# Residual kept in HBM, a second pair of raw-split buffers, and a fixed issue order on two engines, in a float32 encoder block on one Trainium2 core

## The chip, the cores and the metric

The kernel runs on one core of one Trainium2 chip. The time is device microseconds (us) of one execution; it is given as the median of three runs, with the lowest and highest. A profiled execution, recorded by the hardware profiler, has its own time and a span, from the first recorded instruction to the last. The engines are named as in the profile: PE is TensorE (its matmuls; PEld is its weight loads), DVE is VectorE, ACT is ScalarE, POOL is GpSimd and SP is SyncE, which issues the DMAs. L289 means line 289 of the kernel whose profile is shown.

## The reference

One encoder block on x of 256 tokens by 2048 channels, in float32. Cut to what matters:

```python
def swiglu(h, w_gate, w_up, w_down):
    return (jax.nn.silu(h @ w_gate) * (h @ w_up)) @ w_down

for l in range(DEPTH):                                    # DEPTH = 1
    x = x + 0.5 * swiglu(rms_norm(x, ffn1_norm[l]), ffn1_w_gate[l], ffn1_w_up[l], ffn1_w_down[l])
    h = rms_norm(x, mix_norm[l])
    proj = h @ w_in[l]
    ...
    x = x + jnp.concatenate([y_pool, y_gla], axis=-1) @ w_out[l]
    x = x + mem_cross_attention(rms_norm(x, xattn_norm[l]), rms_norm(mem, mem_norm[l]),
                                xattn_w_q[l], xattn_w_kv[l], xattn_w_o[l])
    x = x + 0.5 * swiglu(rms_norm(x, ffn2_norm[l]), ffn2_w_gate[l], ffn2_w_up[l], ffn2_w_down[l])
return rms_norm(x, final_norm)
```

The gate and up weights are 2048 x 5632, the down weights 5632 x 2048. Each value of x is changed seven times by a projection before the last down projection: the residual x is what the change moves.

## The kernel before

**Float32 products out of rounded halves.** PE multiplies values of a shorter float32 form (fp32r in the profile). Each float32 operand is therefore split into a rounded high part and a low remainder, and a product is made of three matmuls: high by high, high by low, low by high. `split` (L215) does this with two instructions: a cast on ACT (L216) and a subtraction on DVE (L217). Activations are split once into `xs` (the normalized x, transposed) or `ys` (the hidden values, transposed); weights are split as they stream in.

**Units.** The weights come in units of 1 MB. A unit u has a raw tile (tag `raw`, three buffers), loaded by SP (L471), and its parts `wh` and `wl` (three buffers each). `Stream.emit` writes the program out: before the matmuls of unit u it calls `prepare(u + 3)`, the split of unit u + 2, and the load of unit u + 5. There are 378 units. Units 0 to 131 are the first feed-forward (FFN1), 246 to 377 the second (FFN2); between them lie the mixer's w_in, w_out (166 to 181), the cross attention and w_o (230 to 245).

**Plain and seven-product units.** A plain unit of a feed-forward (`block_t`, L291, and `unit_p`, L409) has 24 matmuls. Units 0, 2 and 4 of most gate and up blocks of eight units, 54 units in all, save an eighth of them: the 2 x 2 block product is made with seven products in place of eight (`seven`, L367, matmuls at L383), 21 matmuls. Such a unit needs sums of its weight blocks: `add_weights` makes them in tile `T` with three DVE instructions (L345, L348, L349), ahead of the split, in `prepare`. `split_seven` splits T into th and tl, which lie in `wh` and `wl`, and the last three quarters of the raw tile into `xh` and `xl`, which have one buffer each. That second split is a function `rest`, which `emit` calls at the start of the next step, and the load of the raw tile's successor stands behind it.

**A block's end.** A seven-product block needs four accumulators (tiles of PSUM, of which there are four of two banks, tag `ps`). After the last seven-product unit `combine` (L421) moves two of them together into an `sg` tile; after the last unit of the block `join` (L432) adds the other two, and then `ev_gate` applies silu on ACT (L628) or `ev_up` multiplies on DVE (L633). `turn` (L638) transposes a finished half on PE (L643, eight transposes) and splits it into `ys`.

**The feed-forward's order.** `ffn` (L614) goes through three parts of the 5632 hidden columns, (0, 4), (4, 4) and (8, 3) in blocks of 512. A part runs gate and up blocks for two 512-column blocks at a time, g0 u0 g2 u2 in the first part, g4 u4 g6 u6 in the second, g8 u8 and a mixed gate/up block in the third, and then its down projection. In units of FFN1: g0 0 to 7, u0 8 to 15, g2 16 to 23, u2 24 to 31, down 32 to 47, g4 48 to 55, u4 56 to 63, g6 64 to 71, u6 72 to 79, down 80 to 95, and so on. The halves of u0 and u4 are turned six units after their block, so at the end of g2 and g6 (`wait`, L658); the halves of u2 and u6 one unit after theirs.

**The residual.** `X` (L167) holds all of x in SBUF for the whole run, 16 KB in each partition. `residual` (L557) adds the accumulators of a down projection, w_out or w_o into it on DVE (L561). `into_x` (L583) runs two blocks of 1024 columns, b = 0 and 1; where a norm follows, `fold` (L566) transposes the new x on PE into `xs` and takes its squares. The last down projection (`down_end`, L1105) adds, normalizes and stores the output.

**Who sets the order.** A planner places the written instructions on each engine's queue by costs of its own, within what the data allow. An engine then issues its queue in order and waits at an instruction whose inputs are not there. `tc.keep_in_program_order` holds an instruction in the written order with its like. The pools of the scopes (`scope["pool"]`) hold xh, xl, T, `sg` and others; a buffer is taken again when its last reader is done.

Of the kernel before, what the change touches and what calls it, by code (L numbers as in the profile page):

```python
# [7 lines left out]
F32 = mybir.dt.float32  # L8
# [6 lines left out]
P = 128  # L15
D = 2048
# [73 lines left out]
            f(*w.pop(u))  # L90


def build(ctx, tc, I, out):
    nc = tc.nc
    st = Stream()

    head = ctx.enter_context(tc.tile_pool(name="head", bufs=1))
# [22 lines left out]
    def four(ps):  # L120
        return ps.rearrange("p a (b c) -> p (a b) c", c=S)
# [29 lines left out]


    ident = head.tile([P, P], F32, tag="ident", name="ident")
    make_identity(nc, ident)
    ones = const.tile([P, P], F32, tag="ones", name="ones")
    nc.vector.memset(ones, 1.0)
    invc = ctl("invc", [P, PAD])
# [6 lines left out]
    sums = ctl("sums", [P, 2])  # L164
    chain = ctl("chain", [P, 2, 8])

    X = main.tile([P, 2, D], F32, tag="X", name="X")  # L167
    xs = main.tile([P, KT, 2, S], F32R, tag="xs", name="xs")
    ys = main.tile([P, KT, 2, S], F32R, tag="ys", name="ys")

# [51 lines left out]
    def row_squares(src, c):  # L222

        for h in range(2):
            j = tmp.tile([P, S], F32, tag="j", name=uid("j"), bufs=2)
            nc.scalar.activation(j, src[h], AF.Square, accum_out=ss[:, h, c : c + 1])
# [125 lines left out]
    def split_seven(u, raw, t):  # L352
        th, tl = (
            wpool.tile([P, 4 * NB], F32R, tag=n, name=f"{n}{u}", bufs=st.AHEAD + 1)
            for n in ("wh", "wl")
        )
        split(th, tl, t)
        parts = [x.rearrange("p (b n) -> p b n", n=NB) for x in (th, tl)]

        def rest():  # L360
            r = [scope["pool"].tile([P, 3 * NB], F32R, tag=n, name=f"{n}{u}") for n in ("xh", "xl")]
            split(*r, raw[:, NB:])
            parts.extend(x.rearrange("p (b n) -> p b n", n=NB) for x in r)

        return [parts], rest

    def seven(banks, act, ext, i, g, first, later, weights):  # L367
        th, tl, rh, rl = weights
# [150 lines left out]
    def turn_gains(lo, hi):  # L519
        ps = ptile(uid("pgain"))  # L520
        nc.tensor.transpose(ps[:, 0, :P], rows["gain"], ident)
        nc.vector.tensor_copy(gains[:, lo:hi], ps[:, 0, lo:hi])

    def load_x(c):
        cols = slice(c * S, (c + 1) * S)
        nc.sync.dma_start(X[:, :, cols], I["x"][0].rearrange("(h p) d -> p h d", p=P)[:, :, cols])

    def first_load_order():
        for c in range(1, 8):
# [2 lines left out]

    first_loads = first_load_order()

    def x_chunk(c):
        v = ptile(uid("px"))[:, 0, :].rearrange("p (a b) -> p a b", a=2)
        k = 2 * c
        for j in range(2):
            for h in range(2):
                nc.tensor.transpose(  # L540
                    v[:, j, h * P : (h + 1) * P], X[:, h, (k + j) * P : (k + j + 1) * P], ident
                )
        for j in range(2):
            rows["hi", c] = split_scaled(xs, k + j, v[:, j, :], gcol(G_FFN1 + k + j))

    def x_squares(c):
        with tc.issue_after(rows["hi", c].ins):
            row_squares([X[:, h, c * S : (c + 1) * S] for h in range(2)], c)

    def more_gains():  # L550
        gain_columns(
# [2 lines left out]
             ("gla_b_a", G_BA, 4)], nc.sync,  # L554
        )

    def residual(scale, b):  # L557

        def evict(j, ps):
            x = X[:, :, (2 * b + j) * NB : (2 * b + j + 1) * NB]  # L560
            nc.vector.scalar_tensor_tensor(  # L561
                out=x, in0=ps, scalar=scale, in1=x, op0=ALU.mult, op1=ALU.add
            )
        return evict

    def fold(c, gain):  # L566

        v = four(ptile(uid("px")))
        for j in range(4):
            for h in range(2):  # L570
                nc.tensor.transpose(  # L571
                    v[:, j, h * P : (h + 1) * P],
                    X[:, h, c * NB + j * P : c * NB + (j + 1) * P], ident,
                )
        for j in range(4):
            split_scaled(xs, 4 * c + j, v[:, j, :], gcol(gain + 4 * c + j))
        for h in range(2):
            q = tmp.tile([P, NB], F32, tag="j", name=uid("j"), bufs=2)
            nc.scalar.activation(
                q, X[:, h, c * NB : (c + 1) * NB], AF.Square, accum_out=ss[:, h, c : c + 1]  # L580
            )

    def into_x(w, act, scale, gain=None, k0=0, nk=KT, spread_too=True):  # L583

        for b in range(2):
            block_t(wwide(w, b * 2 * NB, k0, nk), act, residual(scale, b))
            if gain is not None:
                for j in range(2):
                    st.op(lambda c=2 * b + j: fold(c, gain), 1)
        if gain is not None:  # L590
            st.op(lambda: finish_norm(4, spread_too), 2)
            if spread_too:
                st.op(spread_norm, 3)
# [14 lines left out]
    class Ext:  # L608


        def __getitem__(self, i):
            return rows["xe"][i]

    def ffn(wg, wu, wd, down):  # L614
        gate = {}

        def hidden():
            e = scope["pool"].tile([P, 4, NB], F32, tag="sg", name=uid("sg"), bufs=2)
# [56 lines left out]
        st.op(lambda c=c: x_squares(c), 6)  # L675
    st.op(lambda: finish_norm(8, False), 7)
    st.op(more_gains, 8)
    st.op(lambda: turn_gains(G_MIX, G_END), 20)

    def down_first(wd, k0, nk, last):  # L680
        into_x(wd, ys, 0.5, G_MIX if last else None, k0, nk)

    for g in PAIRS:
        pair_sums(g, 5)
    ffn(I["ffn1_w_gate"][0], I["ffn1_w_up"][0], I["ffn1_w_down"][0], down_first)
    st.op(close_scope, 1)
    st.op(open_scope("s_mix"), 1)

# [409 lines left out]

    def down_last(wd, k0, nk, last):
        if last:  # L1100
            down_end(wd, k0, nk)
        else:
            into_x(wd, ys, 0.5, None, k0, nk)

    def down_end(wd, k0, nk):  # L1105
# [27 lines left out]

        def end_evict(nb, h):
            cols = slice(nb * NB, (nb + 1) * NB)
            if h == 0 and nb % 2 == 0:
                e = scope["pool"].tile([P, 4, NB], F32, tag="sg", name=uid("O"), bufs=2)
                fin[nb], fin[nb + 1] = e[:, 0:2], e[:, 2:4]
            xn, o = X[:, h, cols], fin[nb][:, h, :]
            nc.vector.scalar_tensor_tensor(  # L1140
                out=xn, in0=acc_ps[nb][:, h, :], scalar=0.5, in1=xn, op0=ALU.mult, op1=ALU.add
            )
            nc.scalar.activation(o, xn, AF.Square, accum_out=ss[:, h, nb : nb + 1])
            if nb < 3 or h == 0:
                nc.gpsimd.tensor_tensor(out=o, in0=xn, in1=fin["gB"][:, cols], op=ALU.mult)
# [4 lines left out]

        def finish(h, c, engine=None):
            cols = slice(c * NB, (c + 1) * NB)
            x, o, r = fin[c][:, h, :], X[:, h, cols], Rcol[:, h : h + 1]
            if h == 1 and c == 3:
                nc.vector.scalar_tensor_tensor(
                    out=o, in0=o, scalar=r, in1=fin["gB"][:, cols], op0=ALU.mult, op1=ALU.mult
                )
            elif engine is nc.scalar:
                nc.scalar.activation(o, x, AF.Copy, scale=r)
            else:  # L1160
                nc.vector.tensor_scalar_mul(o, x, r)
            nc.sync.dma_start(out[0, h * P : (h + 1) * P, cols], o)
# [15 lines left out]

        st.op(ready_sqrt, 8)
        st.op(last_gain, 2)  # L1180
        for b in range(2):
            for i, src in enumerate(wwide(wd, b * 2 * NB, k0, nk - 2)):
                st.unit(src, unit(b, 2 * i))
# [76 lines left out]
```

## Time and profile before

| | |
|---|---|
| runs | 2157.33, 2154.47, 2155.78 us; median 2155.78 |
| profiled execution | 2156.07 us |
| its span | 2154.2 us |
| granted TensorE clock, mean | 0.996 |
| DMA | 404.44 MB, mean 188 GB/s; the hardware queue's packets took 55.8% of 16 engines' span |
| HBM | read 400.80 MB, written 2.10 MB |
| matmul start to start, unhindered | 0.227 us; 5.44 us for 24 matmuls, 4.76 us for 21 |
| first matmul, last matmul's start | 4.1 us, 2144.3 us |

How to read it: a group's row gives the line, the engine, the operation, output and inputs with their shapes, the count, then busy time and the mean of one, then the idle time of the engine just ahead of it and what ended most of that. A row of the waits gives the engine, tile and line that waited, what it waited for, then microseconds in total, times, and the longest. A row of the timeline gives start, duration, engine, line, operation, and in brackets the idle time before it with its releaser. A row of DMA issues gives destination and source, the issuing queue, the count, KB each, and median microseconds from issue to landing. A busy PE is not PE at its peak, since matmuls are pipelined and overlap; the spacing of their starts is the better measure.

### The profile page before, as it was taken

Reading aid. Unit: us, or ns where it says so; the run is one execution under the profiler, and the core shown is the slowest. Engines: PE = TensorE matmul, PEld = TensorE weight load, DVE = VectorE, ACT = ScalarE, POOL = GpSimd, SP = SyncE. Lnnn points to the kernel's source line nnn. Section 1 sums busy time; section 2 is a strip of 40 time slices with the busy share of each in tenths; the row PEclk is TensorE's granted clock in tenths of the full one; section 3 lists DMA queues with packets and bytes.
Section 4 is the critical chain, followed back from the end, with each engine's and each line's share of the span. In section 5 each row is a group of like instructions: output and inputs, shape, how many; then the busy total and the mean of one; then the engine's idle time right before and its main releaser. Section 6 shows DMA issues by size and latency. Waiting matters only on the chain.

```text
span 2154.2 us, 23983 instructions
## 1 busy us (share of the span) xinstructions
PE 2122.0 (99%) x10032; PEld 1771.5 (82%) x10032; DVE 1428.1 (66%) x1189; ACT 1007.4 (47%) x890; POOL 14.1 (1%) x41
## 2 busy tenths in 40 slices
PE   9999999999999999999999999999999999999998
PEld 7878888788888888888888888888878887888886
DVE  8786588756865576565665545567874888658744
ACT  7453354533543545445445434445543445434433
POOL 0000000000000000000000000000000000000001
PEclk9999999999999999999999999999999999999999
DMA  7555555555565555556555555555556554665653
GB/s 274 176 195 200 210 176 192 192 189 192 188 212 186 182 170 179 172 177 198 189 182 166 168 175 157 181 190 197 174 195 195 198 193 170 201 195 197 227 181 117
DMA packets 134675, 404.44 MB, mean 188 GB/s; under 512 B 8868, under 2 KB 12040, under 8 KB 134184
## 3 DMA queue, kind: packets, MB, share of 16 engines
q1 hardware_dynamic: 134536, 402.92, 55.8%
q8 instruction: 78, 1.28, 0.2%
q14 instruction: 29, 0.24, 0.0%
q10 hardware_dynamic: 32, 0.01, 0.0%
HBM read 400.80 MB, written 2.10 MB: 187 GB/s over the span
## 4 chain that ended last, share of the span: by engine, by line
PE 92%; DVE 5%; issue 2%; ACT 1%; DMA 1%; SPq 0%; DVEq 0%; ACTq 0%
PE pt L289 54%; PE pa L274 15%; PE pt L383 10%; PE pb L289 6%; PE pe L289 3%; DVE wl L217 2%; ACT wh L216 1%; PE ph L643 1%; DVE xl L217 1%; DVE T L345 1%; PE pl L1036 1%; PE pv L1071 1%; PE px L571 0%; DVE sg L434 0%; DMA raw<-in_ffn_w_gate 0%
## 5 line engine op out<-in xcount | busy, mean ns | idle before, releaser
L217 DVE TENSOR_TENSOR wl<-raw,wh 128x2048 fp32r<-128x2048 f32 (+2 forms) x328 | 740.2, 2258 | 530.9 <-ACT wh L216 529.9
L216 ACT CAST wh<-raw 128x2048 fp32r<-128x2048 f32 (+2 forms) x329 | 618.4, 1881 | 671.7 <-PE pt L289 471.4
L289 PE MATMUL pt<-wh,xs 128*128 128x512 f32 x1952 | 616.6, 390 | 0.0
L289 PE MATMUL pt<-wh,ys 128*128 128x512 f32 x1728 | 534.6, 389 | 0.0
L289 PEld LDWEIGHTS pt<-wh,xs 128*128 128x128 f32 x1952 | 366.6, 188 | 76.0
L289 PE MATMUL pt<-wl,xs 128*128 128x512 f32 x976 | 380.6, 390 | 0.0
L289 PEld LDWEIGHTS pt<-wh,ys 128*128 128x128 f32 x1728 | 324.1, 188 | 67.0
L289 PE MATMUL pt<-wl,ys 128*128 128x512 f32 x864 | 336.4, 389 | 0.0
L274 PE MATMUL pa<-xs,wh 128*128 128x512 f32 x896 | 318.4, 399 | 1.7 <-DVE t L248 1.7
L274 PE MATMUL pa<-xs,wl 128*128 128x256 f32 x896 | 249.3, 281 | 0.0
L289 PEld LDWEIGHTS pt<-wl,xs 128*128 128x128 f32 x976 | 183.6, 188 | 37.7
L274 PEld LDWEIGHTS pa<-xs,wh 128*128 128x128 f32 x896 | 168.4, 189 | 41.0 <-issue 2.0
L216 ACT CAST wh<-T 128x2048 fp32r<-128x2048 f32 x54 | 103.1, 1909 | 190.0 <-DVE T L349 148.6
L289 PEld LDWEIGHTS pt<-wl,ys 128*128 128x128 f32 x864 | 162.2, 188 | 33.5
L217 DVE TENSOR_TENSOR wl<-T,wh 128x2048 fp32r<-128x2048 f32 x54 | 123.8, 2292 | 88.9 <-ACT wh L216 88.9
L274 PEld LDWEIGHTS pa<-xs,wl 128*128 128x128 f32 x896 | 169.8, 190 | 1.6 <-issue 0.2
L289 PE MATMUL pb<-wh,xs 128*128 128x512 f32 x384 | 121.7, 392 | 0.5 <-DVE ys L209 0.5
L383 PE MATMUL pt<-wh,xe 128*128 128x512 f32 x324 | 114.5, 394 | 2.1 <-DVE ys L217 2.1
L216 ACT CAST xh<-raw 128x1536 fp32r<-128x1536 f32 x54 | 80.0, 1482 | 52.5 <-PE pt L383 22.1
L217 DVE TENSOR_TENSOR xl<-raw,xh 128x1536 fp32r<-128x1536 f32 x54 | 94.6, 1753 | 4.0 <-ACT xh L216 3.7
L289 PEld LDWEIGHTS pb<-wh,xs 128*128 128x128 f32 x384 | 72.1, 188 | 15.6 <-DVE ys L209 0.7
L383 PE MATMUL pt<-xh,xs 128*128 128x512 f32 x216 | 80.3, 396 | 1.5 <-DVE ys L217 1.5
(202 smaller groups left out, 1674.0 us busy)
## 6 DMA issues: line engine op xcount, KB each, us to landing
raw<-in_ffn_w_down SPq DMA_DIRECT2D x88, 1024.0 KB, 5.4
raw<-in_ffn_w_up SPq DMA_DIRECT2D x80, 1024.0 KB, 5.1
raw<-in_ffn_w_gate SPq DMA_DIRECT2D x77, 1024.0 KB, 5.1
raw<-in_w_in SPq DMA_DIRECT2D x32, 1024.0 KB, 5.2
raw<-in_xattn_w_kv SPq DMA_DIRECT2D x32, 1024.0 KB, 5.3
raw<-in_w_out SPq DMA_DIRECT2D x16, 1024.0 KB, 5.6
raw<-in_xattn_w_q SPq DMA_DIRECT2D x16, 1024.0 KB, 5.1
raw<-in_xattn_w_o SPq DMA_DIRECT2D x16, 1024.0 KB, 5.7
```

What stands on the lines that cost most here:

```text
L216: nc.scalar.copy(hi, src)
L217: nc.vector.tensor_tensor(out=lo, in0=src, in1=f32(hi), op=ALU.subtract)
L274: nc.tensor.matmul(o, w, x, start=k == 0 and i == 0, stop=last and i == 1)
L289: nc.tensor.matmul(ps, a, w, start=first and i == 0, stop=last and i == 2)
L345: nc.vector.tensor_tensor(out=v[:, 0:2], in0=w[:, 1:3], in1=w[:, 0:1].to_broadcast([P, 2, NB]), op=ALU.add)
L383: nc.tensor.matmul(banks[n], x, w, start=first and j == 0, stop=not later and n in ("P1", "P5", "P6", "P7") and j == 2,)
L643: nc.tensor.transpose(v[:, i, h * P : (h + 1) * P], g[:, h, i * P : (i + 1) * P], ident)
L1036: nc.tensor.matmul(ps[:, t, :M], ys[:, 4 * h + d, a, tok], xa["K"][:, d, b, :], start=i == 0, stop=i == 11,)
L1071: nc.tensor.matmul(ps[:, d, :S], xa["V"][:, m, a, col], xa["PT"][:, m, b, :], start=i == 0, stop=i == 5,)
```

## The change

It has four parts.

1. *The residual lies in HBM.* `X` becomes two DRAM tiles X0 and X1 of 256 x 1024 float32. `x_tile(b)` takes a tile of 8 KB a partition from tag `sg` of the scope's pool (two buffers). `fetch_x(b)` loads half b of x, as two DMAs of 512 KB on SP's queue, two units into each block of `into_x` (for the first down projection from the input x), and `store_x(b)` writes it back after the second eviction of the half, again two DMAs of 512 KB. At the start the tiles hold the input x for the first norm. In the last down projection both halves are fetched one and three units in, and the output tiles take buffers of xh and xl.
2. *Second buffers for xh and xl*, 6 KB a partition each; `rest` is gone, so both splits of a seven-product unit are written one after the other, and the load of the next raw tile behind them.
3. *A fixed order on DVE and ACT.* `Engines` hands out these two engines wrapped by `Ordered`, which holds every instruction in the written order, from eight units into each feed-forward to the end of FFN1, and in FFN2 to the start of its last down projection. PE, SP and POOL are placed by the planner as before.
4. The second turn of gains (`turn_gains(G_MIX, G_END)`) is due at unit 22 in place of 20.

```diff
@@ -90,8 +90,36 @@
             f(*w.pop(u))
 
 
+class Ordered:
+
+
+    def __init__(self, tc, engine):
+        self.tc, self.engine = tc, engine
+
+    def __getattr__(self, name):
+        f = getattr(self.engine, name)
+
+        def call(*args, **kw):
+            return self.tc.keep_in_program_order(f(*args, **kw))
+
+        return call
+
+
+class Engines:
+
+
+    def __init__(self, tc):
+        self.nc, self.ordered = tc.nc, False
+        self.pinned = {n: Ordered(tc, getattr(tc.nc, n)) for n in ("vector", "scalar")}
+
+    def __getattr__(self, name):
+        if name in ("vector", "scalar") and self.ordered:
+            return self.pinned[name]
+        return getattr(self.nc, name)
+
+
 def build(ctx, tc, I, out):
-    nc = tc.nc
+    nc = Engines(tc)
     st = Stream()
 
     head = ctx.enter_context(tc.tile_pool(name="head", bufs=1))
@@ -164,7 +192,9 @@
     sums = ctl("sums", [P, 2])
     chain = ctl("chain", [P, 2, 8])
 
-    X = main.tile([P, 2, D], F32, tag="X", name="X")
+    dram = ctx.enter_context(tc.tile_pool(name="dram", bufs=1, space=bass.MemoryType.DRAM))
+
+    X = [dram.tile([S, 2 * NB], F32, tag=f"X{b}", name=f"X{b}") for b in range(2)]
     xs = main.tile([P, KT, 2, S], F32R, tag="xs", name="xs")
     ys = main.tile([P, KT, 2, S], F32R, tag="ys", name="ys")
 
@@ -357,12 +387,15 @@
         split(th, tl, t)
         parts = [x.rearrange("p (b n) -> p b n", n=NB) for x in (th, tl)]
 
-        def rest():
-            r = [scope["pool"].tile([P, 3 * NB], F32R, tag=n, name=f"{n}{u}") for n in ("xh", "xl")]
+        if True:
+            r = [
+                scope["pool"].tile([P, 3 * NB], F32R, tag=n, name=f"{n}{u}", bufs=2)
+                for n in ("xh", "xl")
+            ]
             split(*r, raw[:, NB:])
             parts.extend(x.rearrange("p (b n) -> p b n", n=NB) for x in r)
 
-        return [parts], rest
+        return [parts], None
 
     def seven(banks, act, ext, i, g, first, later, weights):
         th, tl, rh, rl = weights
@@ -521,9 +554,21 @@
         nc.tensor.transpose(ps[:, 0, :P], rows["gain"], ident)
         nc.vector.tensor_copy(gains[:, lo:hi], ps[:, 0, lo:hi])
 
+    xrows = {}
+
+    def x_tile(b):
+        xrows[b] = scope["pool"].tile([P, 2, 2 * NB], F32, tag="sg", name=uid("x"), bufs=2)
+        return xrows[b]
+
     def load_x(c):
-        cols = slice(c * S, (c + 1) * S)
-        nc.sync.dma_start(X[:, :, cols], I["x"][0].rearrange("(h p) d -> p h d", p=P)[:, :, cols])
+        b = c // 4
+        if c % 4 == 0:
+            x_tile(b)
+        at = (c % 4) * S
+        nc.sync.dma_start(
+            xrows[b][:, :, at : at + S],
+            I["x"][0].rearrange("(h p) d -> p h d", p=P)[:, :, c * S : (c + 1) * S],
+        )
 
     def first_load_order():
         for c in range(1, 8):
@@ -531,6 +576,11 @@
             yield
 
     first_loads = first_load_order()
+
+    def x_cols(c, n):
+
+        b = c // (2 * NB)
+        return xrows[b][:, :, c - b * 2 * NB : c - b * 2 * NB + n]
 
     def x_chunk(c):
         v = ptile(uid("px"))[:, 0, :].rearrange("p (a b) -> p a b", a=2)
@@ -538,14 +588,14 @@
         for j in range(2):
             for h in range(2):
                 nc.tensor.transpose(
-                    v[:, j, h * P : (h + 1) * P], X[:, h, (k + j) * P : (k + j + 1) * P], ident
+                    v[:, j, h * P : (h + 1) * P], x_cols((k + j) * P, P)[:, h], ident
                 )
         for j in range(2):
             rows["hi", c] = split_scaled(xs, k + j, v[:, j, :], gcol(G_FFN1 + k + j))
 
     def x_squares(c):
         with tc.issue_after(rows["hi", c].ins):
-            row_squares([X[:, h, c * S : (c + 1) * S] for h in range(2)], c)
+            row_squares([x_cols(c * S, S)[:, h] for h in range(2)], c)
 
     def more_gains():
         gain_columns(
@@ -554,35 +604,48 @@
              ("gla_b_a", G_BA, 4)], nc.sync,
         )
 
+    def fetch_x(b, src=None):
+        t = x_tile(b)
+        for h in range(2):
+            rows_h = slice(h * P, (h + 1) * P)
+            nc.sync.dma_start(
+                t[:, h], X[b][rows_h, :] if src is None else src[rows_h, b * 2 * NB : (b + 1) * 2 * NB]
+            )
+
+    def store_x(b):
+        for h in range(2):
+            nc.sync.dma_start(X[b][h * P : (h + 1) * P, :], xrows[b][:, h])
+
     def residual(scale, b):
 
         def evict(j, ps):
-            x = X[:, :, (2 * b + j) * NB : (2 * b + j + 1) * NB]
+            x = x_cols((2 * b + j) * NB, NB)
             nc.vector.scalar_tensor_tensor(
                 out=x, in0=ps, scalar=scale, in1=x, op0=ALU.mult, op1=ALU.add
             )
+            if j:
+                store_x(b)
         return evict
 
     def fold(c, gain):
 
         v = four(ptile(uid("px")))
+        x = x_cols(c * NB, NB)
         for j in range(4):
             for h in range(2):
                 nc.tensor.transpose(
-                    v[:, j, h * P : (h + 1) * P],
-                    X[:, h, c * NB + j * P : c * NB + (j + 1) * P], ident,
+                    v[:, j, h * P : (h + 1) * P], x[:, h, j * P : (j + 1) * P], ident
                 )
         for j in range(4):
             split_scaled(xs, 4 * c + j, v[:, j, :], gcol(gain + 4 * c + j))
         for h in range(2):
             q = tmp.tile([P, NB], F32, tag="j", name=uid("j"), bufs=2)
-            nc.scalar.activation(
-                q, X[:, h, c * NB : (c + 1) * NB], AF.Square, accum_out=ss[:, h, c : c + 1]
-            )
-
-    def into_x(w, act, scale, gain=None, k0=0, nk=KT, spread_too=True):
+            nc.scalar.activation(q, x[:, h], AF.Square, accum_out=ss[:, h, c : c + 1])
+
+    def into_x(w, act, scale, gain=None, k0=0, nk=KT, spread_too=True, src=None):
 
         for b in range(2):
+            st.op(lambda b=b: fetch_x(b, src), 2)
             block_t(wwide(w, b * 2 * NB, k0, nk), act, residual(scale, b))
             if gain is not None:
                 for j in range(2):
@@ -611,8 +674,14 @@
         def __getitem__(self, i):
             return rows["xe"][i]
 
+    def ordered(on):
+        def f():
+            nc.ordered = on
+        return f
+
     def ffn(wg, wu, wd, down):
         gate = {}
+        st.op(ordered(True), 8)
 
         def hidden():
             e = scope["pool"].tile([P, 4, NB], F32, tag="sg", name=uid("sg"), bufs=2)
@@ -675,14 +744,15 @@
         st.op(lambda c=c: x_squares(c), 6)
     st.op(lambda: finish_norm(8, False), 7)
     st.op(more_gains, 8)
-    st.op(lambda: turn_gains(G_MIX, G_END), 20)
+    st.op(lambda: turn_gains(G_MIX, G_END), 22)
 
     def down_first(wd, k0, nk, last):
-        into_x(wd, ys, 0.5, G_MIX if last else None, k0, nk)
+        into_x(wd, ys, 0.5, G_MIX if last else None, k0, nk, src=None if k0 else I["x"][0])
 
     for g in PAIRS:
         pair_sums(g, 5)
     ffn(I["ffn1_w_gate"][0], I["ffn1_w_up"][0], I["ffn1_w_down"][0], down_first)
+    st.op(ordered(False))
     st.op(close_scope, 1)
     st.op(open_scope("s_mix"), 1)
 
@@ -1098,6 +1168,7 @@
 
     def down_last(wd, k0, nk, last):
         if last:
+            st.op(ordered(False), 2)
             down_end(wd, k0, nk)
         else:
             into_x(wd, ys, 0.5, None, k0, nk)
@@ -1133,10 +1204,10 @@
 
         def end_evict(nb, h):
             cols = slice(nb * NB, (nb + 1) * NB)
-            if h == 0 and nb % 2 == 0:
-                e = scope["pool"].tile([P, 4, NB], F32, tag="sg", name=uid("O"), bufs=2)
-                fin[nb], fin[nb + 1] = e[:, 0:2], e[:, 2:4]
-            xn, o = X[:, h, cols], fin[nb][:, h, :]
+            if h == 0:
+                t = scope["pool"].tile([P, 3 * NB], F32, tag=("xh", "xl")[nb % 2], name=uid("O"), bufs=2)
+                fin[nb] = t[:, : 2 * NB].rearrange("p (h n) -> p h n", h=2)
+            xn, o = x_cols(nb * NB, NB)[:, h], fin[nb][:, h]
             nc.vector.scalar_tensor_tensor(
                 out=xn, in0=acc_ps[nb][:, h, :], scalar=0.5, in1=xn, op0=ALU.mult, op1=ALU.add
             )
@@ -1150,7 +1221,7 @@
 
         def finish(h, c, engine=None):
             cols = slice(c * NB, (c + 1) * NB)
-            x, o, r = fin[c][:, h, :], X[:, h, cols], Rcol[:, h : h + 1]
+            x, o, r = fin[c][:, h], x_cols(c * NB, NB)[:, h], Rcol[:, h : h + 1]
             if h == 1 and c == 3:
                 nc.vector.scalar_tensor_tensor(
                     out=o, in0=o, scalar=r, in1=fin["gB"][:, cols], op0=ALU.mult, op1=ALU.mult
@@ -1178,6 +1249,8 @@
 
         st.op(ready_sqrt, 8)
         st.op(last_gain, 2)
+        for b in range(2):
+            st.op(lambda b=b: fetch_x(b), 1 + 2 * b)
         for b in range(2):
             for i, src in enumerate(wwide(wd, b * 2 * NB, k0, nk - 2)):
                 st.unit(src, unit(b, 2 * i))
```

More of the change, by code (lines that the diff above doesn't have):

```diff
@@ L153, in build @@
     ident = head.tile([P, P], F32, tag="ident", name="ident")
-    make_identity(nc, ident)
+    make_identity(tc.nc, ident)
     ones = const.tile([P, P], F32, tag="ones", name="ones")
```

## The prediction, made before the changed kernel was run

> **What bounds the kernel now.** I read the busy times first, then the waits of TensorE (PE), then the start-to-start spacing of its matmuls in the timeline, because a PE row that is "99% busy" says little where matmuls are pipelined.
>
> ```profile
> PE 2122.0 (99%) x10032; PEld 1771.5 (82%) x10032; DVE 1428.1 (66%) x1189; ACT 1007.4 (47%) x890; POOL 14.1 (1%) x41
> ...
> PE pt L383 <- DVE xl L217: 10.7, 5, 2.9
> PE pgain L521 <- DMA gain<-in_ffn_norm: 4.1, 1, 4.1
> PE pt L383 <- DVE ys L217: 3.6, 4, 2.1
> ```
>
> PE is the bound, and nearly all the time it waits is in two rows: seven-product units (line 383) waiting for VectorE (DVE), 14.3 us in nine waits. The 4.1 us is the start of the program, which the change leaves. Matmuls that wait for nothing start 0.227 us apart: 24 of a plain unit 5.44 us, 21 of a seven-product unit 4.76. I went through the starts of the whole trace and summed what exceeds that spacing: 21 us, of which 15.8 lies in the feed-forwards (FFN), all of it where the halves of an earlier gate block are turned at the end of a gate block, so at the hand-over g2 to u2 and g6 to u6 (g = gate, u = up, number = first 512-column part): FFN1 g2 to u2 2.27 + 1.92; FFN1 g6 to u6 0.41 + 0.68 + 3.06; FFN2 0.65 + 3.04 and 0.69 + 3.06. All other seven-product blocks (g4, u4, g8, u8) run at 4.76 and 5.44 exactly. One such place, PE's timeline and then DVE's:
>
> ```profile
> 404.55 0.50 PE L383 MATMUL pt<-xh,xs 128*128 128x512 f32 x1 [0.52 <-DVE ys L217]
> ...
> 414.33 0.39 PE L383 MATMUL pt<-xh,xe 128*128 128x512 f32 x1
> 417.62 0.53 PE L383 MATMUL pt<-xl,xs 128*128 128x512 f32 x1 [2.90 <-DVE xl L217]
> ```
>
> ```profile
> 403.28 1.22 DVE L217 TENSOR_TENSOR ys<-ph,ys 128x1024 fp32r<-128x1024 f32 x1
> 404.41 1.21 DVE L434 TENSOR_TENSOR sg<-pt,sg 128x1024 f32<-128x1024 f32 x1
> 405.55 1.21 DVE L345 TENSOR_TENSOR T<-raw 128x1024 f32<-128x1024 f32 x1
> 406.79 0.69 DVE L348 TENSOR_TENSOR T<-T,raw 128x512 f32<-128x512 f32 x1
> 407.52 0.69 DVE L349 TENSOR_TENSOR T<-T,raw 128x512 f32<-128x512 f32 x1
> 410.27 2.29 DVE L217 TENSOR_TENSOR wl<-T,wh 128x2048 fp32r<-128x2048 f32 x1 [2.06 <-ACT wh L216]
> 412.48 2.28 DVE L217 TENSOR_TENSOR wl<-raw,wh 128x2048 fp32r<-128x2048 f32 x1
> 414.68 1.22 DVE L345 TENSOR_TENSOR T<-raw 128x1024 f32<-128x1024 f32 x1
> 415.81 1.75 DVE L217 TENSOR_TENSOR xl<-raw,xh 128x1536 fp32r<-128x1536 f32 x1
> ```
>
> The reader is to see a late chain: the turned half (ys) and the join delay the sums T; ACT's cast and DVE's wl follow T; a plain unit's wl and the next T's first add still stand ahead of xl, which PE has wanted since 414.56.
>
> **The change, part by part.** The sum is made against the profiled execution: 2156.07 us, span 2154.2 plus 1.9 around it; the three runs' median is 2155.78, so 0.3 lower.
>
> *Order and inlined raw split.* No arithmetic is added on PE, DVE or ACT: the same splits (wl 2.26, xl 1.75, T 1.22 + 2 x 0.69, joins 1.22 each) come in the order th, tl, xh, xl, T, wl. A pair of a seven-product and a plain unit costs DVE 2.29 + 1.75 + 2.59 + 2.26 = 8.89 us, PE 4.76 + 5.44 = 10.20, so DVE has 1.3 us spare per pair. I put the pinned order through a queue by hand with these rows at the four places:
>
> FFN1 g6 to u6 and both of FFN2: in the built order both turns stand before the third-to-last plain unit has run out, so xl of the new block is early; the first accumulator that needs a join's bank wants it 25.3 us after the start of the third seven-product unit of the gate block, and the join ends at 25.1. Stall 0 to 0.2, where there were 4.15, 3.69 and 3.75.
>
> FFN1 g2 to u2: the gains' transpose (moved from unit 20 to 22) takes an accumulator there, and PE makes the second turn only after three matmuls of the last gate unit. From the start of unit 20 that is 4.76 + 2 x 5.44 + 0.9 (first turn) = 16.5, + 0.7 + 0.9 = 18.1; ACT's ys 1.0 and wh 1.9: 21.1; DVE then, in written order, tl 23.5, xl 25.4, T 28.0, wl 30.2, join 31.4. PE starts u2 at 22.9, wants xl at its seventh matmul, 24.3 (waits 1.1), and the joined bank four matmuls later, 26.6 (waits 4.8). Stall 6.0, where there were 4.2.
>
> The same hand queue on the old order gives 2.5 + 1.5 for a measured 2.27 + 1.92, and 0.8 + 2.9 for 0.65 + 3.04, but it also gives 1.9 at a hand-over (g4 to u4) where the trace has none: its error is up to 2 us a place.
>
> *Second xh/xl buffers.* They remove the wait for PE to release the one buffer: ACT's xh row shows it:
>
> ```profile
> L216 ACT CAST xh<-raw 128x1536 fp32r<-128x1536 f32 x54 | 80.0, 1482 | 52.5 <-PE pt L383 22.1
> L345 DVE TENSOR_TENSOR T<-raw 128x1024 f32<-128x1024 f32 x54 | 65.9, 1220 | 3.4 <-DMA raw<-in_ffn_w_up 2.4 <-DMA raw<-in_ffn_w_gate 0.4
> ```
>
> At most 22.1 us of ACT's idle time; ACT is 47% busy and PE did not wait for it, so alone I cost this at nothing. In the timeline above DVE is busy from 410.27 to 418.9 without a gap: xl was late by DVE's order, not by a buffer. [...]
>
> *X in HBM.* Added on SP's queue: 16 fetches and 14 stores of 1 MB, each as two DMAs of 512 KB, 60 DMAs beside the 8 that load x at the start: 30 x 1.05 = 31 MB on 404 MB, so DMA's 56% goes to 60%. The evictions (L561, 28 x 1.22 us) stay as they are. The trace before has no store of this kind. Bounds for one: nothing, if it uses engine time that stands free (44%; the start-up slice moved 274 GB/s against a mean of 188), or 1.05 MB at 188 GB/s = 5.6 us on the landing of one raw load. The loads:
>
> ```profile
> raw<-in_ffn_w_down SPq DMA_DIRECT2D x88, 1024.0 KB, 5.4
> raw<-in_ffn_w_up SPq DMA_DIRECT2D x80, 1024.0 KB, 5.1
> ```
>
> In the down blocks, with three raw buffers, a tile has 3 x 5.44 = 16.3 us from issue to use: 5.4 + 5.6 = 11 is hidden. On SP's queue the fetch of the first half stands near the fifth raw load of its block, the other one load later; the stores stand about three loads into the following block, where the eviction they wait for (2 x 1.22 after the last unit) ends before the next load is due (+4.7). Queued behind them are raw loads, with that 11 - 5.6 = 5 us left. The last stores fall in the next gate block, whose first loads still have the lead of the plain down units. The diagonal tile at the mixer's start and the first sums of FFN2 wait for a store (their addresses come from the x tiles): at most 1 us of DVE, where PE has weights ready. I take 0 to 1 us in all, nearer the low bound, since the rows show DMA engines idle 44% of the time.
>
> **Sum:** 2156.1 - 15.8 + 6.0 + 0.4 (three places at up to 0.2) + 0 to 1 = 2147; as a median 0.3 lower, about **2146**.
>
> **Rivals.**
>
> A, *all stalls go*: the planner still places PE, so it may find the accumulators free at g2 to u2. For: in the three other places the sum is 0. Against: the gains' turn takes one. 2156.1 - 15.8 - 0.3 = **2140**.
>
> C, *raw landings take the gain back*. In the pinned order the load for a seven-product unit is issued after the wl of a plain unit; DVE then has tl and xl (4.04), and T can start only when the load landed: the loop takes max(4.04, L) + 2.59 + 2.26, within 10.20 while L stays under 5.35. The median row is 5.1, and T waited for raw only 3.4 us in all. With L = 6 both pairs of a block run 0.65 over. The three plain units that end it leave DVE 3 x (5.44 - 2.26) = 9.5, of which joins (2.44), combine (2.6) and T (2.59) take 7.6, so the eight gate blocks absorb their 1.3; in the ten up blocks the products take 2.98 more and nothing is left: 13. With L = 5.7 (w_o's row now) it is 7. I take 9: 2146 + 9 = **2155**, no change. [...]
>
> D, *the other side: a written order makes two queues pass on a late PE result*. DVE and ACT can no longer do a later split while a join or a turn waits for PE. Price: at all four late turns what the sum gives for FFN1 g2 to u2, 4 x 6.0 = 24; at the four other gate-to-up hand-overs, where ACT's four silus (2.87) now stand ahead of wh and the third wl is ready 0.2 after it is wanted by my sum, 1.6 each = 6.4; at four up-to-gate ones, where DVE's four products (2.98) do, 0.7 each = 2.8. 33 against 15.8: 2156 + 17 = **2173**. For: margins of 0.2 to 1.3 us, and that the old order already lost 3 us where a queue ran late. Against: g4, u4, g8, u8 lose nothing now in almost the same order. It decides once the FFNs' stalls exceed 20 us.
>
> That the change doesn't do what it says (order the same as before) would leave the nine gaps and give 2156; the built order differs at all four places, so I keep it within C.
>
> **How the numbers follow.** Three runs of before spread by 2.9 us, so 0.2% (4.3 us) is what can be told from no change: faster is under 2151.5, slower over 2160.1. Chances: forecast 0.37, A 0.18, C 0.17, D 0.28. Faster: A, nearly all of the forecast and little of C, 0.55; same: most of C and the edge of D, 0.15; slower: the rest, 0.30. The likeliest's own range is 2141 to 2151 (the 6.0 off by 2 either way, three places of 0 to 2, X 0 to 1). For 8 in 10 the range goes from 2138 (A less its error) to 2168 (the lower part of D).
>
> **What would show it.** Right: PE's waits for xl and ys fall from 14.3 to 5 to 7 us, nearly all before u2 of FFN1; T's wait for raw stays under 5 us, raw rows at 5.1 to 5.5. Wrong by C: T's idle for raw grows over 10 us and its gaps lie inside blocks. Wrong by D: gaps at every hand-over, DVE and ACT idle behind a join or turn whose releaser is PE. By A: no gap over 0.5 us in the FFNs.

## The result and the profile after

| | before | changed |
|---|---|---|
| runs | 2154.47 to 2157.33 us, median 2155.83 (4 runs) | 2141.72 to 2144.98 us, median 2143.14 (4 runs) |
| profiled execution, span | 2156.07, 2154.2 | 2143.86, 2142.1 |
| ratio, 95% interval | | 0.9941 (0.9924 to 0.9959) |

The changed kernel is 0.6% faster. Its page, in the lines that answer to those shown of before:

```profile
span 2142.1 us, 24059 instructions
PE 2117.4 (99%) x10032; PEld 1770.8 (83%) x10032; DVE 1434.5 (67%) x1189; ACT 1004.6 (47%) x890; POOL 14.2 (1%) x41
...
DMA packets 143316, 435.91 MB, mean 203 GB/s; under 512 B 9828, under 2 KB 13000, under 8 KB 142824
...
raw<-in_ffn_w_down SPq DMA_DIRECT2D x88, 1024.0 KB, 5.4
raw<-in_ffn_w_up SPq DMA_DIRECT2D x80, 1024.0 KB, 5.0
```

31 MB more were moved, and the raw loads of the feed-forward weights land as before. PE's waits (microseconds in total, times, longest):

```profile
PE pt L416 <- DVE sg L103: 4.5, 1, 4.5
...
PE pt L319 <- DVE wl L103: 1.4, 1, 1.4
...
PE pt L416 <- DVE xl L103: 0.2, 1, 0.2
```

L416 is the line of the seven products now, L319 that of the plain ones, and L103 is the wrapper of the fixed order, so every DVE or ACT instruction issued in it shows that line. The nine waits for xl and ys, 14.3 us, have shrunk to one of 0.2 for xl. In their place stand one of 4.5 for a join and one of 1.4 for a wl.

To place the difference I went through the starts of the matmuls in each trace again and summed what exceeds the usual spacing. The second number in a cell is the same excess, in us, for matmuls that follow one another at 0.427 us in place of 0.227, behind a gap:

| where, us | before | changed |
|---|---|---|
| FFN1, g2 to u2 | 4.5 + 0.2 | 5.9 + 2.4 |
| FFN1, g6 to u6 | 4.8 + 1.8 | 0.4 |
| FFN1's last down and the mixer's first blocks | 0 | 2.4 |
| FFN2, g2 to u2 | 4.5 + 1.6 | 0 |
| FFN2, g6 to u6 | 4.2 + 2.0 | 0.1 |
| mixer after that | 3.8 + 1.0 | 3.8 |
| first 50 us | 1.7 + 0.6 | 1.8 + 1.6 |

The place that got worse, PE's timeline and then DVE's:

```profile
142.15 0.50 PE L416 MATMUL pt<-xl,xs 128*128 128x512 f32 x1 [0.24 <-DVE xl L103]
...
143.17 0.40 PE L416 MATMUL pt<-wh,xe 128*128 128x512 f32 x1
148.07 0.79 PE L416 MATMUL pt<-xh,xs 128*128 128x512 f32 x1 [4.50 <-DVE sg L103]
```

```profile
136.33 1.23 DVE L103 TENSOR_TENSOR ys<-ph,ys 128x1024 fp32r<-128x1024 f32 x1 [4.21 <-ACT ys L103]
138.13 2.29 DVE L103 TENSOR_TENSOR wl<-T,wh 128x2048 fp32r<-128x2048 f32 x1 [0.58 <-ACT wh L103]
140.34 1.75 DVE L103 TENSOR_TENSOR xl<-raw,xh 128x1536 fp32r<-128x1536 f32 x1
142.01 1.22 DVE L103 TENSOR_TENSOR T<-raw 128x1024 f32<-128x1024 f32 x1
143.26 1.42 DVE L103 TENSOR_TENSOR T<-T,raw 128x512 f32<-128x512 f32 x2
144.60 2.28 DVE L103 TENSOR_TENSOR wl<-raw,wh 128x2048 fp32r<-128x2048 f32 x1
146.80 2.35 DVE L103 TENSOR_TENSOR sg<-pt,sg 128x1024 f32<-128x1024 f32 x2
```

It reads as the prediction wrote it down: DVE sits idle for 4.21 us until the second turned half comes, and then works tl, xl, T, wl and the joins off in the written order, while PE waits for the bank that the first join frees. The sum had 1.1 us of wait for xl and 4.8 for the bank; 0.24 and 4.50 came.

### The profile page after: what moved, and what is told of

The parts are those of the page before. It is cut to its first block, busy times and chain, and to the rows that moved or that the text cites. A ratio compares the mean times of both kernels' runs of the same rounds, so it can differ in the third digit from the quotient of the medians.

```text
span 2142.1 us, 24059 instructions
## 1 busy us (share of the span) xinstructions
PE 2117.4 (99%) x10032; PEld 1770.8 (83%) x10032; DVE 1434.5 (67%) x1189; ACT 1004.6 (47%) x890; POOL 14.2 (1%) x41
## 4 chain that ended last, share of the span: by engine, by line
PE 96%; DVE 2%; ACT 1%; issue 1%; DMA 0%; SPq 0%; DVEq 0%; ACTq 0%
PE pt L319 57%; PE pa L304 15%; PE pt L416 11%; PE pb L319 6%; PE pe L319 3%; PE ph L712 1%; ACT wh L103 1%; PE pl L1106 1%; PE pv L1141 1%; PE px L636 0%; DVE T L103 0%; DVE wl L103 0%; DVE xl L103 0%; DMA x<-in_x 0%; ACT wh L246 0%
## 5 line engine op out<-in xcount | busy, mean ns | idle before, releaser
L319 PE MATMUL pt<-wh,xs 128*128 128x512 f32 x1952 | 618.6, 391 | 0.0
L103 DVE TENSOR_TENSOR wl<-raw,wh 128x2048 fp32r<-128x2048 f32 x186 | 425.1, 2289 | 246.4 <-ACT wh L103 246.4
L319 PE MATMUL pt<-wh,ys 128*128 128x512 f32 x1728 | 535.2, 390 | 0.0
L103 ACT CAST wh<-raw 128x2048 fp32r<-128x2048 f32 x186 | 355.1, 1914 | 378.9 <-PE pt L319 326.5
L247 DVE TENSOR_TENSOR wl<-raw,wh 128x2048 fp32r<-128x2048 f32 (+2 forms) x142 | 314.6, 2216 | 254.5 <-ACT wh L246 254.2
L319 PEld LDWEIGHTS pt<-wh,xs 128*128 128x128 f32 x1952 | 368.0, 189 | 76.3
L246 ACT CAST wh<-raw 128x2048 fp32r<-128x2048 f32 (+2 forms) x143 | 263.1, 1840 | 281.9 <-PE pt L319 96.1
L319 PE MATMUL pt<-wl,xs 128*128 128x512 f32 x976 | 381.3, 391 | 0.0
L319 PEld LDWEIGHTS pt<-wh,ys 128*128 128x128 f32 x1728 | 324.4, 188 | 67.1
L319 PE MATMUL pt<-wl,ys 128*128 128x512 f32 x864 | 336.4, 389 | 1.4 <-DVE wl L103 1.4
L319 PEld LDWEIGHTS pt<-wl,xs 128*128 128x128 f32 x976 | 184.2, 189 | 37.9
L319 PEld LDWEIGHTS pt<-wl,ys 128*128 128x128 f32 x864 | 162.2, 188 | 35.1 <-DVE wl L103 1.9
L103 ACT CAST wh<-T 128x2048 fp32r<-128x2048 f32 x52 | 99.4, 1912 | 151.5 <-PE pt L319 93.2
L103 DVE TENSOR_TENSOR wl<-T,wh 128x2048 fp32r<-128x2048 f32 x52 | 119.0, 2289 | 55.6 <-ACT wh L103 55.2
L319 PE MATMUL pb<-wh,xs 128*128 128x512 f32 x384 | 121.7, 392 | 0.5 <-DVE ys L239 0.5
L416 PE MATMUL pt<-wh,xe 128*128 128x512 f32 x324 | 112.4, 391 | 0.2
L103 DVE TENSOR_TENSOR sg<-pt,sg 128x1024 f32<-128x1024 f32 (+1 forms) x90 | 90.1, 1008 | 6.4 <-ACT sg L103 5.1
L103 DVE TENSOR_TENSOR xl<-raw,xh 128x1536 fp32r<-128x1536 f32 x52 | 91.1, 1751 | 0.0
```

What stands on the lines that cost most here:

```text
L103: return self.tc.keep_in_program_order(f(*args, **kw))
L246: nc.scalar.copy(hi, src)
L247: nc.vector.tensor_tensor(out=lo, in0=src, in1=f32(hi), op=ALU.subtract)
L319: nc.tensor.matmul(ps, a, w, start=first and i == 0, stop=last and i == 2)
L416: nc.tensor.matmul(banks[n], x, w, start=first and j == 0, stop=not later and n in ("P1", "P5", "P6", "P7") and j == 2,)
```

## The experiments

Ten kernels were run, each five rounds beside the kernel before, whose median over these runs lay between 2156.2 and 2156.7. Each line of a diff below is against the changed kernel unless something else is said.

**1. The changed kernel without the fixed order.** DVE and ACT are placed by the planner again; this is called the free order below.

```diff
-        st.op(ordered(True), 8)
```

> The changed kernel without the fixed order on DVE and ACT: the residual in HBM, the second xh/xl buffers and the splits written together stay. Theory O (the order gives the gain): the four hand-overs with late turns lose again what they lost before, 3 to 6 us each in FFN1 g6 to u6 and both of FFN2; time 2152 to 2158. [...]

Measured: 2136.53 us, ratio 0.9908 (0.9895 to 0.9922). It is 6.6 us faster than the changed kernel, whose own ratio to before is 0.9941 (0.9924 to 0.9959), and neither of two theories had that: O, on which the prediction rests, falls, and the time lies 3.5 below the range of B, 2140 to 2146, in which the second buffers give the gain and the gaps at FFN1 g6 to u6 and both of FFN2 stay gone. The rows for ACT's cast to xh, with what ended ACT's idle time ahead of it (microseconds, times); first the one of the kernel before that names PE, then this kernel's:

```profile
  PE pt L383: 22.1, 18
```

```profile
L246 ACT CAST xh<-raw x54: 1469/1484/1489, 38.4 to 1981.4; 128x1536 fp32r<-128x1536 f32 x54
...
  DMA raw<-in_ffn_w_gate: 34.2, 16
  DMA raw<-in_ffn_w_up: 32.9, 19
  PE pt L416: 25.8, 6
```

In the kernel before ACT's idle time ahead of xh ended 18 times with PE, which released the one buffer; here PE ends it six times, and 35 times of 41 it ends when the raw tile lands, so the cast is then made as soon as there is something to cast. The microseconds by themselves don't show it: the six make 25.8, more than the 18 did. What the earlier cast is worth is seen at FFN1 g6 to u6, where the kernel before lost 3.06 us in one gap. The same place, ACT and then DVE:

```profile
391.01 1.49 ACT L246 CAST xh<-raw 128x1536 fp32r<-128x1536 f32 x1 [1.46 <-DMA raw<-in_ffn_w_up]
```

```profile
391.32 0.68 DVE L379 TENSOR_TENSOR T<-T,raw 128x512 f32<-128x512 f32 x1
392.53 1.76 DVE L247 TENSOR_TENSOR xl<-raw,xh 128x1536 fp32r<-128x1536 f32 x1 [0.53 <-ACT xh L246]
394.34 2.29 DVE L247 TENSOR_TENSOR wl<-T,wh 128x2048 fp32r<-128x2048 f32 x1
396.55 1.22 DVE L467 TENSOR_TENSOR sg<-pt,sg 128x1024 f32<-128x1024 f32 x1
```

An xl (392.53) is made ahead of the next joins and the second turned half. In the kernel before DVE sat idle at this place, from 394.57 to 397.74:

```profile
397.74 1.22 DVE L434 TENSOR_TENSOR sg<-pt,sg 128x1024 f32<-128x1024 f32 x1 [3.17 <-PE pt L289]
```

**2. One buffer each for xh and xl, fixed order kept.** The last two output tiles got space of their own.

```diff
-                scope["pool"].tile([P, 3 * NB], F32R, tag=n, name=f"{n}{u}", bufs=2)
+                scope["pool"].tile([P, 3 * NB], F32R, tag=n, name=f"{n}{u}", bufs=1)
```

> The changed kernel with one buffer each for xh and xl; fixed order and residual in HBM stay; the last two output tiles get space of their own. Theory O: ACT's cast to xh waits for PE to finish the previous seven-product unit, then xh 1.48 and xl 1.75 are done 3.3 us into the plain unit between (5.44), so PE waits for nothing new: 2142 to 2147. Theory B: in a fixed order everything behind that cast waits too; the gaps come back at each pair of seven-product units, 36 in all, 2150 or more.

Measured: 2149.31 us, 0.9965 (0.9951 to 0.9978), between the two theories: slower than the changed kernel by 6.2, still faster than before by some 7. Waits come back, but not at each of the 36 pairs: beside the place at FFN1 g2 to u2 and one wait of 0.9 for a join, PE waits eight times for ACT's wh, 2.5 us in all. Experiment 10 follows these eight.

**3. The fixed order alone, residual in SBUF.** Against the kernel before: the fixed order, the splits written together, the turn at 22; no second buffers, no HBM.

```diff
-        def rest():
+        if True:
...
-        return [parts], rest
+        return [parts], None
...
+        st.op(ordered(True), 8)
```

> The kernel before with the fixed order, the two splits of a seven-product unit written together and the gains' turn at 22, but with the residual in SBUF and one buffer each for xh and xl. Against e2_one_buffer it shows what the residual's 60 transfers cost by themselves. Theory O: same as e2 within 1.5 us. Rival (transfers beside raw loads take time): this one is 3 us or more below e2. Theory B: 2150 or more, since neither buffers nor space are there.

Measured: 2148.23 us, 0.9963 (0.9950 to 0.9975). Against experiment 2 the residual's transfers cost 1.1 us by the medians, and the intervals don't tell them apart.

**4. The gains' turn later.**

```diff
-    st.op(lambda: turn_gains(G_MIX, G_END), 22)
+    st.op(lambda: turn_gains(G_MIX, G_END), 36)
```

> The changed kernel with the second turn of gains due at unit 36, in the first down projection, where a plain block leaves two accumulators free, in place of 22. Theory: in FFN1 g2 to u2 it was the accumulator that this turn takes that let PE make the second half's turn only inside the last gate unit. Without it the 5.4 us of gaps there and the 2.9 us of matmuls at half the spacing rate behind them go: 2143 - 8 = 2135, range 2134 to 2138. Rival: the late turn is the planner's choice and the queue is late anyway, 2141 to 2144.

Measured: 2133.43 us, 0.9893 (0.9880 to 0.9907); 9.7 us below the changed kernel. The theory held, with a time 0.6 below its range. The turns at the end of g2 on PE, in the changed kernel and then in this one:

```profile
127.05 0.27 PE L554 MATMUL pgain<-ident,gain 128*128 128x128 f32 x1
128.78 1.03 PE L712 MATMUL ph<-ident,sg 128*128 128x128 f32 x8
134.21 1.04 PE L712 MATMUL ph<-ident,sg 128*128 128x128 f32 x8
```

```profile
126.13 1.91 PE L712 MATMUL ph<-ident,sg 128*128 128x128 f32 x16
```

With the gains out of the way both halves are turned together, 8 us before the changed kernel turns its second, and FFN1 g2 to u2 has no gap left. That the turn stands in the way through the accumulator it takes is read from the kernel, where both are tiles of tag `ps`; the run shows that moving the turn clears the place.

**5 and 6. What of the free order's gain comes from the buffers.** Both against experiment 1: number 5 with one buffer each (the edit of experiment 2), number 6 with the raw split written a step late again, as in the kernel before (`rest`), and two buffers.

> As e1_free_order (no fixed order, residual in HBM, splits written together), but one buffer each for xh and xl. Theory B2 (in free order the second buffers give the gain, since xl of the next block's first unit can then be made in the quiet stretch ahead of the hand-over): the gaps at the hand-overs with late turns come back, 2150 to 2157. Rival W (writing the two splits together, with the next load right behind, gives it): stays at 2135 to 2140.

> As e1_free_order with both buffers, but the raw split written a step later again, as in the kernel before (the function rest). Theory B2: stays at 2134 to 2140, for the buffers are there. Rival W: 2148 or more.

Measured: 2156.93 us, ratio 1.0000 (0.9991 to 1.0010), for number 5, and 2137.50 us, 0.9910 (0.9896 to 0.9924), for number 6. B2 holds in both, W in neither. Number 5's waits show the old gaps again:

```profile
PE pt L416 <- DVE xl L247: 11.5, 7, 2.9
...
PE pt L416 <- DVE ys L247: 3.6, 4, 2.1
```

**7. The fixed order ended before FFN1's last down projection.** Against experiment 4:

```diff
     def down_first(wd, k0, nk, last):
+        if last:
+            st.op(ordered(False), 2)
```

> e4_gains_later with the fixed order ended two units into FFN1's last down projection in place of its end, so the planner may lay the folds' 16 short pairs between weight splits again. Theory: the 1.6 us gap before wl and the 0.6 at the mixer's first blocks go, 2.2 us: 2133.4 - 2.2 = 2131, range 2130 to 2132.5. Rival: the gap comes from the x stores on SP's queue, nothing changes, 2133 to 2134.

Measured: 2132.65 us, 0.9890 (0.9876 to 0.9904), 0.8 below experiment 4 where 2.2 was expected; the runs alone don't separate the two. The traces show the place cleared: gaps from 700 to 760 us fall from 2.4 to 0.7. Their spans, 2132.5 and 2130.5, differ by more, but the profiled execution of experiment 4 was the longest of its four. The 1.6 before wl is gone, the 0.6 at the mixer's first blocks stays. In the changed kernel the place looks so, ACT's rows:

```profile
704.48 0.47 ACT L103 ACTIVATE xs<-px,gains 128x256 fp32r<-128x256 f32 x1 [4.41 <-PE px L636]
705.50 0.47 ACT L103 ACTIVATE xs<-px,gains 128x256 fp32r<-128x256 f32 x1 [0.55 <-DVE xs L103]
...
713.82 5.50 ACT L103 CAST wh<-raw 128x2048 fp32r<-128x2048 f32 x3
```

Two folds in written order go back and forth between ACT and DVE, 1.03 us a piece of x, and no weight is split from 704.5 to 713.8. PE then waits 1.44 us for a wl. The free planner lays the splits between the pieces: in the kernel before ACT casts to wh at 704.88 and at 712.11 us, with pieces of x between the two and behind the second.

**8. Free order, the gains' turn at 36.** Experiments 1 and 4 together.

> e1_free_order with the gains' turn at unit 36. Theory: in free order the turn at 22 costs little (0.7 us of gaps at FFN1 g2 to u2), so 2135.5 to 2136.5; beside e4_gains_later (2133.4) it shows what the fixed order is worth once buffers and turn are settled: 2 to 3 us. Rival: the fixed order is worth nothing, 2132.5 to 2134.

Measured: 2136.02 us, 0.9906 (0.9892 to 0.9920). As the theory had it: in free order the turn costs nothing that the runs show, and the fixed order, rid of its bad place, is ahead by 2.6 us (2132.9 to 2134.3 in the runs of experiment 4, 2134.8 to 2137.7 here; the intervals of the two ratios overlap). The trace has a place for it: in free order PE waits twice for ACT's wh, 1.7 us in all, near 366 and 1767 us, each with about 1.5 us by the spacing of starts; experiment 4 has no such wait.

**9. The residual's transfers doubled.** Against experiment 7, every fetch and store issued twice, which changes no value.

```diff
-        for h in range(2):
+        for h in (0, 1, 0, 1):
```

> e7_order_ends_early with every fetch and every store of the residual (not the first loads of x) issued twice, so another 31 MB on the queue. Theory (the transfers lie beside raw loads that have time to spare): 2132.6 + 0 to 2. Rival (they stretch the raw loads that the sums T wait for): T's wait for raw grows well over the 11 us of the changed kernel and the time by 5 or more.

Measured: 2132.37 us, 0.9893 (0.9879 to 0.9906), no different from experiment 7, at 467 MB in place of 436:

```profile
DMA packets 151956, 467.37 MB, mean 219 GB/s; under 512 B 10788, under 2 KB 13960, under 8 KB 151464
...
L103 DVE TENSOR_TENSOR T<-raw 128x1024 f32<-128x1024 f32 x50 | 61.0, 1220 | 9.9 <-DMA raw<-in_ffn_w_gate 5.5 <-DMA raw<-in_ffn_w_up 4.4
```

**10. The fixed order with one buffer, the gains' turn at 36.** Experiment 3 with the edit of experiment 4.

> e3_order_in_sbuf (fixed order, one buffer each, residual in SBUF) with the gains' turn at 36. Theory: the 8.5 us of gaps and slow matmuls at FFN1 g2 to u2 go, 2148.2 - 8 = 2140, range 2138.5 to 2141.5; what is left of them against e4_gains_later (2133.4) is the price of one buffer under the fixed order, some 7 us against the 20 of the free order. Rival: with one buffer the place loses its 4 us of gaps whatever the turn does, 2143 to 2146.

Measured: 2140.49 us, 0.9931 (0.9917 to 0.9944). The theory held. What is left against experiment 4 is in one row, eight waits at the second seven-product unit of the gate blocks, for ACT's cast of the sums T:

```profile
PE pt L411 <- ACT wh L103: 2.5, 8, 0.3
```

By the spacing of starts these eight places lose some 0.96 us each, 7.7 together, and the medians differ by 7.1. In g4 the cast of T began at 283.99 us, and in experiment 4 at 279.89. The steps are in the trace, ACT's row and then DVE's:

```profile
278.02 1.48 ACT L103 CAST xh<-raw 128x1536 fp32r<-128x1536 f32 x1 [5.79 <-PE pt L411]
```

```profile
279.54 1.76 DVE L103 TENSOR_TENSOR xl<-raw,xh 128x1536 fp32r<-128x1536 f32 x1 [4.94 <-ACT xh L103]
281.21 1.22 DVE L103 TENSOR_TENSOR T<-raw 128x1024 f32<-128x1024 f32 x1
```

ACT has to wait for PE's last read of the only xh, which began at 277.55; DVE waits for that cast, and in the written order T stands behind xl. With two buffers (experiment 4) the same cast began at 271.28 and T at 275.33.

The medians in one table:

| us | one buffer | two buffers |
|---|---|---|
| free order, turn at 22 | 2156.9 | 2136.5 |
| free order, turn at 36 | not tried | 2136.0 |
| fixed order, turn at 22 | 2149.3 (residual in SBUF: 2148.2) | 2143.1, the changed kernel |
| fixed order, turn at 36 | 2140.5 (residual in SBUF) | 2133.4; ended early: 2132.7 |

The best version is experiment 7, 10.5 us below the changed kernel and 23.6 below the 2156.2 of the kernel before beside it.

## Why the prediction came out right, and where its reasons did not

**The sum.** 2147 was forecast for the profiled execution and 2143.86 came. The direction and the size are right, and so are the terms of the order's step: no stall at three hand-overs (0.4, 0 and 0.1 us of gaps), and 6.0 at FFN1 g2 to u2, where the gaps were 5.9. That the total came so near is in part luck. The same sum holds for a kernel with the fixed order alone, since buffers and residual stood in it at next to nothing, and that kernel (experiment 3) took 2148.2. The buffers' 6.2 us under the fixed order (experiment 2 against the changed kernel) were not in the sum, nor were the terms below that it left out.

**The step that failed** is "alone I cost this at nothing", said of the second buffers. They are worth 20 us in free order (experiments 1 and 5) and 6 to 7 under the fixed one (6.2 between experiment 2 and the changed kernel, 7.1 between 10 and 4). I looked at the busy stretch in which xl was late, saw that DVE had no gap there, and concluded that no buffer was missing. The missing buffer acted earlier: the only xh was held by PE's matmuls of the seven-product unit before, whose last read is this row:

```profile
409.23 0.39 PE L383 MATMUL pt<-xh,xe 128*128 128x512 f32 x1
```

So xl could not be made in the idle 3.17 us that ended at 397.74, and had to join the busy stretch. Its raw tile was not what held it: that load was issued at 387.73 us, and in experiment 1, where it was issued at 385.16, the cast to xh could begin on it 5.9 us later. The row of ACT's idle time released by PE pointed there by its 18 times, not by its 22.1 us, since 25.8 of such time are left in experiment 1, where the gaps are gone.

**The order's credit.** I gave the order all of the 15.8 us. Alone it brings 8.5 (experiment 3), and 15.7 once the gains' turn is moved (10). With the buffers there it is worth 2.6 with the turn at 36 and costs 6.6 with the turn at 22. The two parts remove the same gaps, so their gains don't add: my forecast hit because the order by itself also clears three of the four places (in experiment 3's trace they have 0.1 to 0.2 us of gaps and one slow matmul each).

**FFN1 g2 to u2** came out for the reason given. The gains' turn takes an accumulator, the second half is turned late, and a fixed queue hands that on. Free order (experiment 1) loses 0.7 there with the same late turn, since DVE makes the next xl ahead of the ys; without the late turn (4) the fixed order loses nothing.

**The residual in HBM**, 0 to 1 us: held, by experiments 2 and 3 (1.1, within the intervals), by the doubling (9), and by experiment 5, which has the residual in HBM, free order and one buffer, and a ratio of 1.0000 to the kernel before.

**Terms that I left out.** Matmuls 0.427 us apart behind the long gaps cost the kernel before 5.4 us in the three places that were cleared, and the changed kernel 2.4 at g2 to u2. FFN1's last down projection, with the two folds, and the mixer's first blocks cost 2.4; 1.7 of it goes when the fixed order ends ahead of the folds (experiment 7). The start and the mixer moved by +1.1 and -1.0. Together with the gaps, 13.5 less 0.5 at the cleared places and 1.4 more at g2 to u2: -13.0 - 5.4 + 1.4 + 2.2 + 2.4 + 0.1 = -12.3, of 12.2 that the last matmul starts earlier; small gaps outside the table are some tenths.

**The rivals.** A, that all stalls go, came true at three places; at g2 to u2 the buffers clear it too in free order (0.6 us of waits for ys are left in experiment 1), and the fixed order keeps it. C's marker showed without its effect, and against the forecast's own sign of under 5 us: T's wait for raw tiles rose from 3.4 to 12.2 us (11.5 and 0.7), but it is 1.1 in the free order with the same traffic and no larger with the traffic doubled, so it comes from the fixed order, and PE did not wait for it. Of the landings, w_out's raw loads took 6.2 us in place of 5.6; they took 6.2 in experiment 5 too, whose ratio is 1.0000. D, queues that pass on a late PE result, acted at two places, g2 to u2 and the folds, not at twelve.

## What to carry to other kernels

A resource that is missing shows where it could have been used earlier, not where the queue is late: look for idle time on the engine ahead of its busy stretch, and ask what kept the late instruction out of it. Two parts that remove the same wait should be tried alone before either is credited, and a part that looks harmless can take from the other. A fixed issue order is worth what the planner's own order loses, and each place at which it holds an instruction for a late result, a turn or a chain of short pairs, has to be looked at by itself.

## What the runs showed of the hardware

In the feed-forwards of these two traces each gap of 3 us or more on PE cost more than its length: 3.06, 3.04 and 3.06 us in the kernel before were followed by 1.8, 1.6 and 2.0 us of excess in slow matmuls, 4.67 us in the changed kernel by 2.4. The granted clock in windows of the kernel before, and then of the changed one (window; PE, PEld, DVE, ACT and POOL busy with counts; granted clock; DMA share; GB/s):

```profile
414.00:417.60 3.60, 0.72 (x4) 0.25 (x2) 3.60 (x4) 0.00 (x0) 0.00 (x0) 1.00 0.47 118
417.60:421.40 3.80, 3.78 (x10) 2.99 (x11) 1.72 (x3) 2.40 (x2) 0.00 (x0) 0.55 0.99 385
421.40:425.00 3.60, 3.60 (x17) 2.98 (x16) 3.60 (x3) 2.77 (x2) 0.00 (x0) 1.00 0.14 58
```

```profile
148.00:153.60 5.60, 5.53 (x13) 4.37 (x14) 2.26 (x3) 5.49 (x6) 0.00 (x0) 0.50 0.56 186
153.60:158.00 4.40, 4.40 (x19) 3.58 (x19) 4.37 (x4) 2.05 (x2) 0.00 (x0) 0.95 0.11 16
```

Behind the gaps of 3.06 and 4.67 us, with matmuls 0.427 us apart, the clock was 0.55 from 417.6 to 421.4 us and 0.50 from 148.0 to 153.6 us. Behind gaps of 2.27 and 1.92 us in the kernel before it was 1.00 (142 to 146 and 155.7 to 160 us). The length of a gap alone doesn't decide it: in the mixer PE waited 1.01 and 1.65 us among small products in both kernels, and behind the second wait the clock was 0.59 from 919 to 923 us in the kernel before and 1.00 from 920.2 to 924.2 us in the changed one. What made the difference there is not shown.
